# A hybrid encoder on Trainium2: filler moved from first to second half heads of the scan, outputs spread over more places

## The chip, the cores and the metric

One core of a Trainium2 chip runs the whole kernel. TensorE (PE) multiplies and transposes, VectorE (DVE) and ScalarE (ACT) work on elements, GpSimd (POOL) does small vector work and issues some transfers, SyncE (SP) issues most DMAs. The engines run side by side, each through its own queue in order, and wait for each other on semaphores. The metric is the device time of one execution in microseconds, taken as the median of several runs.

## The reference, cut to what matters

One layer over 1024 positions of width 1024: an RMS norm, one combined projection, a convolution mixer and a bidirectional gated recurrence (HGRN2) side by side, their gated merge, and a feed-forward block with a short convolution. The change is in the recurrence, which runs for 8 heads of dimension 128, once forward and once backward:

```python
def step(state, inp):                       # one chunk of positions
    ...
    scores = jnp.einsum("bhtk,bhsk,bhtsk->bhts", qb, kb, decay)
    o = (jnp.einsum("bhts,bhsv->bhtv", scores, vb)
         + jnp.einsum("bhtk,bhkv->bhtv", qb * jnp.exp(a), state))
    ...
o = o_fwd + o_bwd                           # [B,S,H,DV]
of = o * lax.rsqrt(jnp.mean(o * o, axis=-1, keepdims=True) + EPS)
bmix = of * norm_w * jax.nn.silu(og)
```

## The kernel before

Large products run in three float32r passes (L144, L145, L146): each weight page and each activation page is split into a high and a low part, ACT writing the high part (L122) and DVE the low one (L119). The stages follow each other: norm and first projections, convolution beside projections, the recurrence ("the scan", about 530 to 960 us of the profile), output projection and merge, feed-forward, final norm.

**The scan.** It treats each of the 8 heads in two halves of 512 positions (four chunks of 128), first half, then second. In a half:

- `scan_base` (L875) prepares qF and kG, the scaled queries and keys of both directions, with VectorE alone. It is a generator of twelve steps, run a half ahead of use (`ahead`).
- `scan_levels` (L935) joins blocks at four levels, h = 8, 16, 32 and 64. At each, ACT copies keys into A (L945), PE makes eight products, two recorded for each of four chunks (L948), ACT or DVE puts them into the score tile S (L972, L975 to L979, L983), and DVE updates kG and qF for the next level (through `tt`, L840). Level 8 has the products inside the blocks too (L961). A yield follows each level. Ahead of the third place PE transposes v (L1151).
- `scan_states` (L997) transposes kG (L1004; ACT copies the result to kT, L1006), then forms the state contributions u = kT v (L1013) and, on DVE, the forward states Sf (L1021). ACT copies u for the backward states Sb (L1031, L1033). Three yields.

So a half has seven yields, here called **places**, and a head fourteen. At each place `between` does three things in this order: `dense.fill(FILL)`, two steps of the next half's `scan_base`, and one step of `pending`.

- `dense` is the remaining column jobs of the input projection, there to keep PE busy. One column job is eight **pieces** of six products (L144 to L146), then evacuations by ACT (L544, L546) and stores; its weight page is loaded by SP and split by ACT and DVE. `fill(1.3)` adds 1.3 to what is owed and runs one piece for each whole unit, so the seven places of a half bring 9.1 pieces on average. What is left of the jobs after the scan is run behind it.
- `pending` is the generator `outputs` (L1102) of the head before. Its steps are: Sb's recursion, six dependent DVE instructions (L1106); the output products of the first half, 22 on PE into bank "ob" (L1054), copied by ACT (L1056) and squared there (L1059); the same for the second half, then the reciprocal root on POOL (`rstd_small`, L408 and L409); an empty step; the scalings by ACT, four for each half (L1073), in two steps; and for each half four transpositions on PE (L1080), a DVE product with the gate (L1082) and a store. With one step at each place, step k falls in place k of the next head: the last transpositions are done in the first place of its second half. In head 0 there is nothing pending.

**What sets the order.** PE's order is that of the program as written; the other engines' instructions are put in order by the framework's scheduler, from the program's order and its own estimates. PSUM has eight banks: three "mm" for the column jobs, two "sc", two "tr" for transpositions, and one "ob", used by half of level 8's inner products, by half of u, and by the output products. Buffers for a head's states (tag "st") are four, so the next head writes Sf and Sb into the buffers that the outputs read.

After the loop stands a tail written out by hand: calls of `pending.fill` and `dense.fill` for the last head's outputs, and `bm_loads`, which load what the output projection needs.

Of the kernel before, what the change touches and what calls it, by code (L numbers as in the profile page):

```python
# [16 lines left out]
AX = mybir.AxisListType  # L17

P = 128
FILL = 1.3  # L20
CONV_FILL = 1.6
NPAIRS = 17
LN_FILL = 6
# [22 lines left out]
def tile_hybrid_encoder(  # L46
# [45 lines left out]
    def nm(s):  # L92
        uid[0] += 1
        return f"{s}_{uid[0]}"
# [3 lines left out]
    def bank(tag):  # L98
        return ps.tile([P, H], F32, tag=tag, name=nm(tag), bufs=BANKS[tag])

    def page(pool, tag, bufs, dt=F32):
        return pool.tile([P, H], dt, tag=tag, name=nm(tag), bufs=bufs)

    def tmp():
        return page(mp, "tm", 4)

    def ev():
        return page(mp, "ev", 3)

    def hx():  # L110
        return page(mp, "hx", 32, F32R)

    def load(src):
        t = tmp()
        nc.sync.dma_start(t, src)
        return t
# [4 lines left out]
    def split(hi, lo, src, eng):  # L121
        A.copy(hi, src)  # L122
        split_lo(eng, lo, src, hi)
        return hi, lo
# [248 lines left out]
    def vec(key, i):  # L373
        name, o = vec_off[key]
        return vecs[name][:, o + i : o + i + 1]
# [31 lines left out]
    def rstd_small(dst, ss, n):  # L407
        G.tensor_scalar(dst, ss, 1.0 / n, EPS, op0=ALU.mult, op1=ALU.add)  # L408
        G.tensor_tensor(dst, dst, mhalf.to_broadcast(list(dst.shape)), op=ALU.pow)  # L409
# [441 lines left out]
    def scan_inputs(i):  # L851


        h, half = divmod(i, 2)
        q = page(hp, "q", 2)
        f = hp.tile([P, 2, H], F32, tag="f", name=nm("f"), bufs=2)
        kk = hp.tile([P, 2, H], F32, tag="k", name=nm("k"), bufs=2)
        nc.sync.dma_start(q, d_q[h][half])
        for d in range(2):
            z = page(hp, "zi", 3)  # L860
            nc.sync.dma_start(z, d_z[d][h][half])
            A.activation(kk[:, d, :], z, AF.Sigmoid, scale=-1.0)
            A.activation(z, z, AF.Sigmoid)
            fo = view(f, d * H + 7 * d, [[8, NB], [1 - 2 * d, 8]])
            A.activation(
                fo,
                z.rearrange("p (b e) -> p b e", e=8),
                AF.Identity,
                scale=oml_of(d, h),
                bias=lb_of(d, h),  # L870
            )
        V.tensor_scalar(f, f, MIN_FORGET, 1.0, op0=ALU.max, op1=ALU.min)
        return q, f, kk, kscale[:, h : h + NH + 1 : NH]
# [162 lines left out]
    def scan_outputs(h, kept, Sf, Sb):  # L1036


        ons, gates = [], []
        ss = cp.tile([P, 2, 4], F32, name=nm("oss"), tag="oss", bufs=2)  # L1040
        rs = cp.tile([P, 2, 4], F32, name=nm("ors"), tag="ors", bufs=2)
        for half in range(2):
            S_t, v, qF = kept[half]
            o = bank("ob")
            for c in range(4):
                sl = slice(c * P, (c + 1) * P)
                g = half * 4 + c
                terms = [(S_t[:, c, :], v[:, c, :])]
                if g > 0:
                    terms.append((qF[:, 1, sl], Sf[half][:, c, :]))  # L1050
                if g < 7:
                    terms.append((qF[:, 0, sl], Sb[half][:, c, :]))
                for n, (l, r) in enumerate(terms):
                    T.matmul(o[:, sl], l, r, start=(n == 0), stop=(n == len(terms) - 1))  # L1054
            on = tmp()
            A.copy(on, o)  # L1056
            for c in range(4):
                junk = hp.tile([P, DK], F32, tag="jk", name=nm("jk"), bufs=1)
                A.activation(  # L1059
                    junk, on[:, c * P : (c + 1) * P], AF.Square, accum_out=ss[:, half, c : c + 1]  # L1060
                )
            ons.append(on)
            gates.append(page(hp, "og", 2))
            nc.sync.dma_start(gates[half], d_og[h][half])
            if half == 0:
                yield
        rstd_small(rs, ss, DK)
        yield
        yield
        for half in range(2):  # L1070
            for c in range(4):
                sl = slice(c * P, (c + 1) * P)
                A.activation(  # L1073
                    ons[half][:, sl], ons[half][:, sl], AF.Copy, scale=rs[:, half, c : c + 1]
                )
            yield
        for half in range(2):
            b = bank("tr")
            for c in range(4):
                T.transpose(b[:, c * P : (c + 1) * P], ons[half][:, c * P : (c + 1) * P], ident)  # L1080
            bt = ev()
            V.scalar_tensor_tensor(bt, b, vec("hn", h), gates[half], op0=ALU.mult, op1=ALU.mult)  # L1082
            if h == NH - 1:
                bm[h][half] = split(hx(), hx(), bt, V)
            else:
                nc.sync.dma_start(d_bm[h][half], bt)
            yield
# [13 lines left out]

    def outputs(h, kept, Tt, Sf, Sb):  # L1102
        for c in range(5, -1, -1):
            hf, cc = c // 4, c % 4
            n1, c1 = (c + 1) // 4, (c + 1) % 4
            V.scalar_tensor_tensor(  # L1106
                Sb[hf][:, cc, :],
                Sb[n1][:, c1, :],
                Tt[:, n1, 1, c1 : c1 + 1],
                Sb[hf][:, cc, :],  # L1110
                op0=ALU.mult,
                op1=ALU.add,
            )
        yield
        yield from scan_outputs(h, kept, Sf, Sb)
# [11 lines left out]
    pending = Stream(iter(()))  # L1127
    for h in range(NH):
        Tt = hp.tile([P, 2, 2, 4], F32, tag="Tt", name=nm("Tt"), bufs=3)
        Sf = [hp.tile([P, 4, DK], F32, tag="st", name=nm("Sf"), bufs=4) for _ in range(2)]  # L1130
        Sb = [hp.tile([P, 4, DK], F32, tag="st", name=nm("Sb"), bufs=4) for _ in range(2)]
        kept = []
        for half in range(2):
            i = 2 * h + half
            base = cur.result()
            ahead = Base(ins) if i + 1 < NI else None
            ins = scan_inputs(i + 2) if i + 2 < NI else None

            def between(fill):
                dense.fill(fill)  # L1140
                if ahead is not None:
                    ahead.step(BASE_STEPS)
                pending.fill(1)

            S_t = hp.tile([P, 4, P], F32, tag="S", name=nm("S"), bufs=3)
            vl = load(d_v[h][half])
            for n, _ in enumerate(scan_levels(base, S_t, Tt[:, half])):
                if n == 2:
                    b = bank("tr")
                    for c in range(4):  # L1150
                        T.transpose(b[:, c * P : (c + 1) * P], vl[:, c * P : (c + 1) * P], ident)  # L1151
                    v = hp.tile([P, 4, DK], F32, tag="v", name=nm("v"), bufs=3)
                    A.copy(v.rearrange("p c e -> p (c e)"), b)
                between(FILL)
            qF, kG = base[0], base[1]
            for _ in scan_states(i, kG, v, Tt, Sf, Sb):
                between(FILL)
            kept.append((S_t, v, qF))
            cur = ahead
        pending = Stream(outputs(h, kept, Tt, Sf, Sb))  # L1160

    left = 8 * (len(rest) - 2) + 16 - dense.count
    pending.fill(1)
    dense.fill(left - 20)
    pending.fill(1)
    dense.fill(4)
    pending.fill(2)
    dense.fill(4)
    pending.fill(2)
    dense.fill(4)  # L1170
# [323 lines left out]
```

## Time and profile before

| | |
|---|---|
| median of 3 runs | 1859.93 us (1857.55 to 1863.16) |
| the profiled execution | 1873.26 us |
| its span, first to last instruction | 1871.5 us |
| granted TensorE clock, mean | 0.984 of full speed |
| busy: PE, DVE, ACT, POOL | 1788.6, 1275.7, 796.2, 185.8 us |
| matmuls | 8574 |

The profiled execution is one of its own and 13 us longer than the median. Durations below come from it. "Busy" is the time in which an engine had at least one instruction under way; for PE the ends of matmuls are modelled, so its figure is somewhat high. In the views, a wait is written as the waiting engine, tile and line, then the engine, tile and line that released it.

### The profile page before, as it was taken

The page shows a single profiled execution, that of the slowest core. Times are in us where ns is not written, and L with a number is a line of the kernel's source. Part 1 is how long each engine was busy: PE and PEld are TensorE (multiplying, and loading weights), DVE is VectorE, ACT ScalarE, POOL GpSimd, SP SyncE. Part 2 cuts the span into 40 slices and gives each one's busy share as a digit, 9 for nine tenths or more (in the row PEclk, how much of TensorE's full clock was granted, in tenths as well). Part 3 has the DMA queues.
Part 4 walks back from the last instruction along what each step waited for, and adds up shares of the span by engine and source line. Part 5 has one row for each costly group of instructions (what it writes and reads, how often), then busy time and mean ns, then how long its engine had stood idle before and what let it go on. Part 6 is the DMA issues. An engine that isn't in the chain of part 4 may idle for free.

```text
span 1871.5 us, 23768 instructions
## 1 busy us (share of the span) xinstructions
PE 1788.6 (96%) x8574; PEld 1481.4 (79%) x8574; DVE 1275.7 (68%) x1874; ACT 796.2 (43%) x1483; POOL 185.8 (10%) x197
## 2 busy tenths in 40 slices
PE   7989999999999999999989999899999999899996
PEld 6868777777778888888878787688888888788885
DVE  4599999534479999999835565666666667534445
ACT  6443333234545566556442244443444434522124
POOL 1201111213000000000000001111111111000000
PEclk9999999999999999999999999999999999999998
DMA  7658878775653333332238665676776765633134
GB/s 268 213 141 185 184 170 198 184 170 130 208 186 96 113 113 117 98 108 91 74 110 239 191 193 190 152 156 144 150 153 149 156 146 130 208 97 95 55 86 169
DMA packets 323468, 281.42 MB, mean 150 GB/s; under 512 B 14734, under 2 KB 246934, under 8 KB 323350
## 3 DMA queue, kind: packets, MB, share of 16 engines
q1 hardware_dynamic: 272886, 240.05, 41.4%
q0 software_dynamic: 50464, 39.85, 14.9%
q8 instruction: 67, 1.10, 0.3%
q14 instruction: 51, 0.42, 0.1%
HBM read 188.09 MB, written 71.83 MB: 139 GB/s over the span
## 4 chain that ended last, share of the span: by engine, by line
PE 45%; DVE 23%; DMA 18%; ACT 6%; issue 5%; POOL 1%; SPq 0%; ACTq 0%; POOLq 0%; DVEq 0%
PE mm L144 12%; PE mm L145 12%; PE mm L146 12%; DMA wr<-wr 4%; DVE wp L119 3%; DMA wr<-sw 3%; DMA sw<-in_w_in_dram 3%; DMA tm<-d_a 3%; DVE kG L840 2%; DVE acc L755 2%; PE sc L144 2%; PE sc L146 2%; PE sc L145 2%; DVE qF L840 2%; DVE DE L840 2%
## 5 line engine op out<-in xcount | busy, mean ns | idle before, releaser
L144 PE MATMUL mm<-hx,wp 128*128 128x512 f32 x1176 | 480.1, 408 | 23.8 <-DVE ev L541 6.8
L146 PE MATMUL mm<-hx,wp 128*128 128x512 f32 x1176 | 464.9, 395 | 1.9 <-DVE wp L119 1.9
L145 PE MATMUL mm<-hx,wp 128*128 128x512 f32 x1176 | 464.6, 395 | 0.5 <-DVE hx L476 0.5
L122 ACT CAST wp<-wr 128x1024 fp32r<-128x1024 f32 (+2 forms) x193 | 176.7, 915 | 344.8 <-PE mm L145 188.3
L119 DVE TENSOR_TENSOR wp<-wr,wp 128x1024 fp32r<-128x1024 f32 (+2 forms) x193 | 203.4, 1054 | 123.0 <-ACT wp L122 116.2
L144 PEld LDWEIGHTS mm<-hx,wp 128*128 128x128 f32 x1176 | 224.7, 191 | 72.9 <-DVE ev L541 9.7
L146 PEld LDWEIGHTS mm<-hx,wp 128*128 128x128 f32 x1176 | 224.1, 191 | 52.5 <-DVE wp L119 3.7
L145 PEld LDWEIGHTS mm<-hx,wp 128*128 128x128 f32 x1176 | 224.7, 191 | 43.0 <-DVE hx L476 0.8
L755 DVE SCALAR_TENSOR_TENSOR acc<-gl,v_b,acc 128x1024 f32<-128x1024 f32 x120 | 150.0, 1284 | 0.5
L1370 DVE TENSOR_TENSOR xr<-mm,xr 128x512 f32<-128x512 f32 x48 | 33.1, 690 | 80.4 <-PE mm L146 80.4
L948 PE MATMUL sc<-qF,A 128*128 128x128 f32 x512 | 69.8, 280 | 13.3 <-DVE qF L840 13.1
L948 PEld LDWEIGHTS sc<-qF,A 128*128 128x128 f32 x512 | 65.2, 195 | 20.4 <-issue 14.9
L242 POOL DMA_DIRECT2D wr<-sw x38 | 33.8, 889 | 442.8 <-DVE wp L119 153.1
L122 ACT CAST wq<-sw 128x1024 fp32r<-128x1024 f32 x39 | 41.0, 1051 | 77.1 <-PE mm L145 59.5
L945 ACT COPY A<-kG 128x512 f32<-128x512 f32 x64 | 39.6, 618 | 73.8 <-DVE kG L840 51.3
L1292 DVE SCALAR_TENSOR_TENSOR tm<-gp,v_a,tm 128x512 f32<-128x512 f32 x88 | 65.6, 746 | 3.3 <-ACT tm L1288 2.5
L144 PE MATMUL mm<-hy,wp 128*128 128x512 f32 x156 | 62.2, 399 | 3.1 <-ACT su L270 2.9
L145 PE MATMUL mm<-hy,wp 128*128 128x512 f32 x156 | 61.9, 396 | 0.7 <-DVE hy L119 0.7
L270 ACT COPY su<-mm 128x512 f32<-128x512 f32 x78 | 45.1, 578 | 39.2 <-PE mm L146 39.2
L144 PE MATMUL tr<-hx,wp 128*128 128x512 f32 x156 | 61.4, 394 | 0.0
L146 PE MATMUL mm<-hy,wp 128*128 128x512 f32 x156 | 61.1, 392 | 0.0
L144 PE MATMUL sc<-hy,wq 128*128 128x512 f32 x156 | 61.1, 392 | 0.0
(322 smaller groups left out, 3601.5 us busy)
## 6 DMA issues: line engine op xcount, KB each, us to landing
wr<-in_w_in_dram SPq DMA_DIRECT2D x53, 512.0 KB
sw<-in_ffn_w_up_dram SPq DMA_DIRECT2D x44, 256.0 KB
sw<-in_ffn_w_up_dram POOLq DMA_DIRECT2D x22, 512.0 KB, 9.2
wr<-in_ffn_w_up_dram SPq DMA_DIRECT2D x22, 512.0 KB
d_g<-ft SPq DMA_DIRECT2D x44, 256.0 KB
ev<-d_g SPq DMA_DIRECT2D x44, 256.0 KB
wr<-sw POOLq DMA_DIRECT2D x38, 256.0 KB, 3.2
wr<-wr POOLq DMA_DIRECT2D x38, 256.0 KB, 4.8
```

What stands on the lines that cost most here:

```text
L119: eng.tensor_tensor(lo, src, hi.bitcast(F32), op=ALU.subtract)
L122: A.copy(hi, src)
L144: T.matmul(acc, whi[:, k, :], ahi, start=first, stop=False, skip_group_check=again)
L145: T.matmul(acc, whi[:, k, :], alo, start=False, stop=False, skip_group_check=again)
L146: T.matmul(acc, wlo[:, k, :], ahi, start=False, stop=last, skip_group_check=again)
L242: G.dma_start(o, a, accum_op=ALU.add)
L270: A.copy(t, acc)
L755: V.scalar_tensor_tensor(acc, g[:, k : k + S], tap(k), acc, op0=ALU.mult, op1=ALU.add)
L840: V.tensor_tensor(o, a, b, op=op)
L945: A.copy(A_t.rearrange("p (b x e) -> p b x e", x=2, e=h), pairs(kG, h))
L948: T.matmul(b[:, c * P : (c + 1) * P].rearrange("p (b x e) -> p b x e", x=2, e=h), A_t[:, c * P : (c + 1) * P], view(qF, c * P, [[2 * h, P ...
L1292: V.scalar_tensor_tensor(c, g[:, o + k : o + k + H], vec("fdw", k * NF + j), c, op0=ALU.mult, op1=ALU.add,)
```

## The change

Three things. `FILL` becomes a pair, 1.1 for the places of a first half and 1.5 for those of a second. `outputs` yields once within Sb's recursion, after three of its six instructions, so that the recursion takes two places. And the empty steps between the reciprocal root and the scalings become three (four yields in place of two), so that the outputs of a head take eleven of the next head's fourteen places: recursion in places 1 and 2, output products in 3 and 4, nothing in 5 to 7, scalings in 8 and 9, transpositions in 10 and 11. The tail's calls of `pending.fill` are raised by the added steps, and the same work stands between the same calls of `dense.fill` as before.

```diff
-FILL = 1.3
+FILL = (1.1, 1.5)
...
         rstd_small(rs, ss, DK)
-        yield
-        yield
+        for _ in range(4):
+            yield
         for half in range(2):
...
     def outputs(h, kept, Tt, Sf, Sb):
         for c in range(5, -1, -1):
+            if c == 2:
+                yield
             hf, cc = c // 4, c % 4
...
-                between(FILL)
+                between(FILL[half])
             qF, kG = base[0], base[1]
             for _ in scan_states(i, kG, v, Tt, Sf, Sb):
-                between(FILL)
+                between(FILL[half])
...
-    pending.fill(1)
+    pending.fill(2)
     dense.fill(left - 20)
     pending.fill(1)
     dense.fill(4)
-    pending.fill(2)
+    pending.fill(4)
     dense.fill(4)
     pending.fill(2)
     dense.fill(4)
```

## The prediction

> **What bounds the kernel now.** I read the engines' totals first, then the busy time per half head of the scan (the change touches nothing outside it but the order of some hand-written calls behind it), then who makes TensorE wait there, and last the timeline around those waits.
>
> ```profile
> PE 1788.6 (96%) x8574; PEld 1481.4 (79%) x8574; DVE 1275.7 (68%) x1874; ACT 796.2 (43%) x1483; POOL 185.8 (10%) x197
> ```
>
> Over the whole span TensorE (PE) is the bound and VectorE (DVE) is far from it. The scan is different. I cut it at the first level-8 product of each half head; a row has start:end, length, then busy us (and count) of PE, PE's weight loads, DVE, ACT and POOL, the granted clock, DMA share and GB/s. Odd rows are first halves, even ones second halves of heads 0 to 7.
>
> ```profile
> 547.40:573.30 25.90, 23.06 (x132) 19.89 (x131) 23.99 (x42) 10.66 (x19) 0.00 (x0) 0.93 0.35 109
> 573.30:595.70 22.40, 21.36 (x131) 18.48 (x130) 22.33 (x46) 12.36 (x23) 0.00 (x0) 1.00 0.28 87
> 595.70:623.20 27.50, 26.56 (x180) 23.89 (x179) 23.39 (x44) 16.24 (x44) 1.85 (x2) 1.00 0.25 77
> 623.20:647.30 24.10, 21.86 (x137) 18.91 (x136) 23.99 (x43) 13.84 (x25) 0.00 (x0) 1.00 0.46 143
> 647.30:675.20 27.90, 27.02 (x180) 23.91 (x178) 25.31 (x51) 16.45 (x45) 1.87 (x2) 1.00 0.26 85
> 675.20:698.70 23.50, 21.93 (x135) 18.83 (x136) 22.90 (x40) 11.74 (x22) 0.00 (x0) 1.00 0.40 120
> 698.70:726.00 27.30, 26.53 (x179) 23.84 (x178) 25.36 (x51) 17.39 (x46) 2.55 (x2) 1.00 0.35 108
> 726.00:749.60 23.60, 21.66 (x137) 18.87 (x136) 23.18 (x41) 12.66 (x24) 0.00 (x0) 1.00 0.43 136
> 749.60:777.60 28.00, 26.67 (x180) 23.96 (x179) 25.19 (x51) 17.25 (x46) 1.83 (x2) 1.00 0.27 85
> 777.60:804.00 26.40, 24.51 (x142) 21.19 (x141) 24.48 (x45) 11.56 (x22) 0.00 (x0) 0.94 0.37 110
> 804.00:831.80 27.80, 26.76 (x179) 23.77 (x178) 24.60 (x48) 18.00 (x47) 1.84 (x2) 1.00 0.26 86
> 831.80:854.40 22.60, 21.69 (x137) 18.91 (x136) 22.50 (x39) 11.50 (x22) 0.00 (x0) 1.00 0.41 129
> 854.40:882.00 27.60, 26.51 (x180) 23.86 (x179) 24.67 (x48) 17.17 (x46) 1.83 (x2) 1.00 0.21 67
> 882.00:905.10 23.10, 21.61 (x137) 18.85 (x136) 22.97 (x41) 8.77 (x17) 0.00 (x0) 1.00 0.35 116
> 905.10:931.80 26.70, 26.55 (x180) 23.90 (x179) 21.11 (x45) 14.34 (x41) 2.02 (x2) 1.00 0.18 59
> 931.80:955.00 23.20, 21.94 (x138) 18.99 (x136) 13.18 (x24) 6.90 (x13) 0.00 (x0) 1.00 0.35 114
> ```
>
> Take heads 1 to 6, which are alike (595.70 to 905.10, 309.4 us). A first half lasts 27.68 on average, PE is busy 26.68 of it, DVE 24.75, ACT 17.08: PE bounds it, 1.0 us is lost. A second half lasts 23.88, PE is busy 22.21, DVE 23.34, ACT 11.68: DVE bounds it, and PE stands idle 1.7 us. The two halves have different bounds, and each leaves the other engine's time unused. All that PE loses in these heads is 6 x (1.0 + 1.7) = 16.1 us; that is the ceiling of what any reordering can win there.
>
> Who PE waits for between 595 and 905 (total us, times, longest), and two waits of ACT between 547 and 955:
>
> ```profile
> PE sc L948 <- DVE qF L840: 8.8, 8, 1.9
> PE sc L1013 <- ACT kT L1006: 5.5, 6, 1.3
> PE sc L961 <- ACT Sb L1031: 1.5, 1, 1.5
> ```
>
> ```profile
> ACT k L862 <- DVE Kh L843: 15.4, 8, 3.9
> ACT tm L1073 <- POOL ors L409: 9.2, 7, 1.6
> ```
>
> The three rows sum to 15.8 us, the same idle time seen from the other side. The second occurs six times, once per first half. The timeline of head 2's first half shows its origin:
>
> ```profile
> 670.25 1.28 ACT L1073 ACTIVATE tm<-tm,ors 128x128 f32<-128x128 f32 x4 [1.37 <-POOL ors L409]
> 671.44 0.56 ACT L1006 COPY kT<-tr 128x512 f32<-128x512 f32 x1
> 672.97 1.23 DVE L119 TENSOR_TENSOR wp<-wr,wp 128x1024 fp32r<-128x1024 f32 x1 [2.49 <-ACT wp L122]
> ```
>
> ACT stands 1.37 us at the output scaling (L1073) until POOL has the reciprocal root, spends 1.28 us on four scalings, and only then copies kT, for which PE waits; a weight page behind it on ACT is late too, and DVE idles 2.49 us for that.
>
> **The change part by part.** Durations (us busy, mean ns; the last row min/median/max ns):
>
> ```profile
> L1106 DVE SCALAR_TENSOR_TENSOR Sb<-Sb,Tt 128x128 f32<-128x128 f32 x38 | 13.1, 344 | 0.5 <-ACT Sb L1031 0.3
> L1082 DVE SCALAR_TENSOR_TENSOR ev<-tr,v_a,og 128x512 f32<-128x512 f32 x14 | 10.4, 744 | 1.7 <-PE tr L1080 1.7
> L119 DVE TENSOR_TENSOR wp<-wr,wp 128x1024 fp32r<-128x1024 f32 x18 | 21.9, 1219 | 7.0 <-ACT wp L122 7.0
> L1073 ACT ACTIVATE tm<-tm,ors 128x128 f32<-128x128 f32 x56 | 17.9, 391 | 9.2 <-POOL ors L409 9.2
> L1056 ACT COPY tm<-ob 128x512 f32<-128x512 f32 x14 | 8.1, 577 | 9.4 <-PE ob L1054 9.4
> L409 POOL TENSOR_TENSOR ors<-ors,mhalf x8: 1633/1634/1669, 616.9 to 964.5; 128x8 f32<-128x8 f32 x8
> ```
>
> What PE does around level 32 in a first half (head 1), with the DVE update that this level needs, and in a second half (head 4):
>
> ```profile
> 599.79 1.05 PE L948 MATMUL sc<-qF,A 128*128 128x128 f32 x8
> 600.60 0.47 PE L144 MATMUL mm<-hx,wp 128*128 128x512 f32 x1
> 602.02 0.67 DVE L840 TENSOR_TENSOR qF<-qF,tb 128x512 f32<-128x512 f32 x1
> 602.07 0.38 PE L1054 MATMUL ob<-v,S 128*128 128x128 f32 x2
> 604.52 1.06 PE L948 MATMUL sc<-qF,A 128*128 128x128 f32 x8
> ```
>
> ```profile
> 783.04 0.60 PE L1080 MATMUL tr<-ident,tm 128*128 128x128 f32 x4
> 783.47 1.06 PE L948 MATMUL sc<-qF,A 128*128 128x128 f32 x8
> 787.81 1.13 PE L948 MATMUL sc<-qF,A 128*128 128x128 f32 x8 [1.89 <-DVE qF L840]
> 790.08 0.63 PE L146 MATMUL mm<-hx,wp 128*128 128x512 f32 x1
> ```
>
> *Filler.* Per half 1.3 x 7 = 9.1 pieces become 1.1 x 7 = 7.7 and 1.5 x 7 = 10.5; a head keeps 18.2, so the scan's total, and what is left for the tail, stay. A piece is six products, 600.60 to 602.07 = 1.47 us, or about 1.4 where it follows another. So 1.4 pieces, 1.95 us of PE, move. A column job has eight pieces and one DVE subtraction of 1.22 us (L119): 0.21 us of DVE moves with them, and the jobs' loads and stores move on SP's queue with their piece, whose DMA share here is 0.18 to 0.46.
>
> *Turning the outputs (places 10 and 11).* Before, one transposition block was in the last place of a first half and one in the first of a second; now both are in the second, places 3 and 4. That moves 783.04 to 783.47 = 0.43 us of PE and one L1082, 0.74 us of DVE.
>
> *Scalings (places 8 and 9).* Eight go from the end of a first half to the start of a second: two groups of 1.28 us, 2.6 us of ACT. POOL's 1.63 us now has three empty places ahead of its reader; even three single pieces are 4.4 us, so the 1.37 us wait on POOL should go. If POOL were later than that, the wait would come back at the second half's first levels.
>
> *Sb's recursion.* Six steps of 0.34 us stay six; three go one place later, so up to 1.0 us of DVE moves from ahead of level 16 to ahead of level 32. The output products, which read Sb, go a place later too.
>
> *New per half, heads 1 to 6.* First half: PE 26.68 - 1.95 - 0.43 = 24.3, DVE 24.75 - 0.74 - 0.21 = 23.8, ACT 17.08 - 2.6 = 14.5 or a little less. Second half: PE 22.21 + 2.38 = 24.6 (24.1 without the half at 777.60, which has a slow clock), DVE 23.34 + 0.95 = 24.3, ACT 14.3. Both halves are balanced; neither engine has two us to spare any more. What is lost above the busiest engine is 1.0 us now in a first half (27.68 - 26.68) and 0.5 in a second (23.88 - 23.34). With two engines level, it can't be less; from 0.5 to the 2.7 us that PE loses per head now are the bounds per half. I take 1.0 for a first half (its kT wait goes, a wait at level 32 comes) and 0.5 for a second: 25.3 + 25.1 = 50.4 against 51.56, 1.2 us a head, 7 us in six heads.
>
> *Where cover is lost.* In a first half the 22 output products (602.07 to 604.52, 2.45 us) stood between level 16 and level 32; now they stand behind level 32, and mostly one piece of 1.4 us is left as cover. DVE's update began at 602.02, 0.67 long: with the level wanted at 602.1 instead of 604.5, PE would wait some 0.6 us here, up to 1.9 as in the second halves. In a second half both L1082 (1.5 us of DVE) and, on average, one filler piece less stood ahead of level 32; I expect the 1.89 us waits there to go mostly. I cost this pair at +0.8 and -1.2 us a head; it lies within the sums above.
>
> *New waits.* The two output blocks share one ob bank and are now only level 64 (0.8 us, as level 16 from 599.79 to 600.60) and one piece apart: the copy L1056 (0.58 us) must leave ACT within some 2.3 us, and ACT has waits of up to 3.9 us (L862) that could stand ahead of it. Behind it wait PE's second block, and all that follows on PE. In places 3 to 6 of a second half, v's, two output and two kT transpositions take the two tr banks in turn: kT then waits for L1082 on DVE. Bounds: nothing, to 1.3 us a head (the longest wait for kT now). I take nothing for the tr banks, as two places lie between, and 0.2 us for ob.
>
> *Heads 0 and 7.* Head 0 has no outputs to spread. Its first half loses two pieces, but is late through DVE (23.99 of 25.90): -0.3; its second gains two, PE 21.36 + 2.8 = 24.2, with 0.5 lost 24.7 against 22.40: +2.3. In head 7 DVE has room in both halves (21.11, 13.18), PE sets both, and work only changes sides: 0. The tail has the same order on PE.
>
> *The slow spell.* After the 1.89 us wait at 787.81 a product takes 0.63 us (790.08) where 0.47 and less is usual, and that half's granted clock is 0.94; the other second halves of heads 1 to 6 have 1.00. Its PE time is 24.51 against 21.75 on average in the other five, and the sums above carry these 2.8 us. I take it that the wait brought the spell and that both go: -2.8. An execution that had no such spell before gains that much less.
>
> Sum: -7.0 + 0.2 x 6 + 2.0 - 2.8 = **-6.6 us**. The profiled execution took 1873.26 us, its span and 1.8 us around it; the median of the runs shown is 1859.93. The scan's rows hold for both, so 1873.26 becomes 1866.7, and the median 1859.93 - 6.6 = **1853 us**.
>
> **The rivals.** *The slow spell stays* (1856): if a wait as short as 1.89 us doesn't slow the clock, the spell at 790 has another cause and comes again; -6.6 + 2.8 = -3.8. For it: seven of the eight waits for qF between 595 and 905 are followed by no spell. The Trainium skill ("TensorE: Matmul & The Clock Gate", "Part 1: The HAM clock gate") has the clock halve after about 3.4 us of idling, and by that page waits of this length cost no clock. The trace agrees in those seven places and not in the one.
>
> *Balanced and none the better* (1859): two level engines wait for each other as much as before, 2.7 us of PE a head, only elsewhere; six heads then give nothing, and head 0's +2 and the spell's -2.8 leave -1. For it: now an engine with 1.9 us of room (26.68 against 24.75) stands beside the bound one in a first half, and none after. Against it: kT's wait has a cause that is removed. *The change doesn't reach its waits* belongs here: if kT is held up by the squares of the second block, which now stand one place later, instead of the scalings, 5.5 us stay.
>
> *Level 32 in first halves* (1867): DVE must do Sb's six steps, 2.06 us, ahead of that level as before, but PE arrives 2.45 us earlier. If DVE enters a first half no earlier than now, PE waits 8.8 / 8 = 1.1 (the mean wait for qF, mostly in second halves) + 2.06 = 3.2 us there, first half 24.3 + 3.2 = 27.5, second 24.6 + 0.5 = 25.1: 52.6 against 51.56, +6; with head 0's +2.0 and a half of the spell's -2.8, +7. It decides once PE's waits pass 2.7 us a head. Against it: a second half's DVE is no longer the bound by 1.6 us, so it should enter the next first half earlier.
>
> *Most of PE's idle time goes* (1846): 0.5 us lost in each half, first 24.3 + 0.5, second 24.6 + 0.5: 49.9 a head, 1.66 less, -10; with head 0's +2.0 and the spell's -2.8, -11, and up to -14 where DVE's late start in head 0 goes too.
>
> **How the numbers follow.** A measurement of this kernel tells 0.3% (5.6 us) from no change. Forecast 0.32, most idle time goes 0.22, the spell stays 0.06, balanced 0.20, level 32 0.20. The forecast's own spread reaches to about -4, so 0.02 of it lies within 0.3%: faster 0.32 + 0.22 - 0.02 = 0.52, within 0.3% 0.06 + 0.20 + 0.02 = 0.28, slower 0.20. The range takes in all five: from 1841 (all of the 16.1 us and the spell gone, head 0 as above: -17, and 2 us more for the runs' own spread) to 1868 (level 32).
>
> **What would show it.** Right: rows of first and second halves within 1 us of each other, near 25; no row of L1073 waiting for POOL in the scan; PE's wait for kT under 2 us in all, for qF under 9 spread over both halves; DVE over 0.95 busy in both. Wrong: first halves still at 27 with qF waits at level 32; L1054 waiting for L1056, or L1004 for L1082; ACT's copies of kT still late.

## The result and the profile after

| | before | after |
|---|---|---|
| median of 5 runs | 1861.05 us (1857.55 to 1864.15) | 1880.14 us (1873.10 to 1882.42) |
| ratio | | 1.0096 [1.0071, 1.0120] |
| profiled execution, its span | 1873.26, 1871.5 us | 1878.54, 1876.8 us |

The changed kernel is slower. On a second occasion (run e5 below) the same two kernels gave 1.0051 [1.0033, 1.0069], 9.7 us. I cut the two traces at the first inner product of the scan (L961) and its last state product (L1013): the scan takes 404.3 us before and 413.4 after, 9.1 more. What comes behind it takes about 919 in both; over the profiles of all kernels here that part, whose work is the same, lies between 903 and 919. So about 9 us are the scan's, by one profile of each kernel, and the other 9 or 10 of the first occasion are not explained by any row that I found.

The engines' totals of after, which hardly differ from those of before:

```profile
PE 1787.7 (95%) x8574; PEld 1477.7 (79%) x8574; DVE 1280.1 (68%) x1874; ACT 795.1 (42%) x1483; POOL 185.7 (10%) x197
```

The half heads of heads 1 to 6 of after, cut and read as the prediction's view of before (first halves in the odd rows):

```profile
590.00:616.80 26.80, 24.93 (x163) 22.41 (x163) 24.97 (x50) 14.34 (x37) 1.74 (x2) 0.94 0.29 89
616.80:644.60 27.80, 25.07 (x151) 21.59 (x150) 25.39 (x46) 16.14 (x33) 0.10 (x1) 1.00 0.34 105
644.60:672.80 28.20, 26.32 (x170) 23.54 (x169) 23.00 (x43) 14.26 (x39) 2.03 (x2) 0.94 0.27 84
672.80:698.20 25.40, 23.48 (x145) 20.47 (x144) 24.36 (x42) 14.24 (x30) 0.00 (x0) 1.00 0.44 139
698.20:724.90 26.70, 24.72 (x169) 22.27 (x169) 25.25 (x51) 14.21 (x38) 1.83 (x2) 1.00 0.30 95
724.90:750.80 25.90, 23.76 (x146) 20.53 (x145) 23.27 (x42) 14.72 (x31) 0.00 (x0) 1.00 0.37 123
750.80:776.50 25.70, 25.01 (x169) 22.21 (x168) 24.51 (x50) 13.66 (x37) 1.83 (x2) 1.00 0.28 93
776.50:804.00 27.50, 25.08 (x151) 21.58 (x150) 24.99 (x46) 14.82 (x32) 0.00 (x0) 1.00 0.35 106
804.00:828.10 24.10, 23.36 (x163) 21.18 (x162) 23.34 (x44) 13.51 (x37) 1.83 (x2) 1.00 0.31 100
828.10:855.30 27.20, 25.02 (x151) 21.58 (x151) 25.12 (x44) 16.17 (x33) 0.00 (x0) 1.00 0.31 107
855.30:880.00 24.70, 23.37 (x164) 21.17 (x163) 23.71 (x48) 13.60 (x36) 1.13 (x2) 1.00 0.19 64
880.00:910.60 30.60, 27.81 (x151) 24.09 (x150) 25.76 (x48) 11.27 (x25) 1.43 (x1) 0.89 0.29 95
```

The mean of six rows of a kind: a first half lasts 26.0 us with PE busy 24.6, DVE 24.1, ACT 13.9; a second half 27.4 with 25.0, 24.8 and 14.6. The work moved as forecast (24.3, 23.8, 14.5 and 24.6, 24.3, 14.3). The loss above PE did not: 1.4 us in a first half (1.0 forecast) and 2.4 in a second (0.5 forecast). The six heads take 320.6 us instead of 309.4. Who PE waits for there (between 588 and 908), and ACT's wait for POOL in the whole scan (540 to 960):

```profile
PE sc L948 <- DVE qF L840: 10.4, 7, 2.0
PE sc L961 <- ACT Sb L1031: 9.4, 6, 2.7
PE sc L948 <- ACT ev L544: 1.4, 1, 1.4
PE tr L1004 <- ACT kT L1006: 0.8, 1, 0.8
PE sc L1013 <- ACT kT L1006: 0.6, 1, 0.6
```

```profile
ACT tm L1073 <- POOL ors L409: 12.2, 7, 2.3
```

The kT waits are gone (0.6 of 5.5 us), as forecast. In their place stands a row that was 1.5 us, once: the inner products of level 8 wait for the copy of Sb, 9.4 us in six. And the wait on POOL, which the prediction saw go, grew from 9.2 to 12.2. All rows sum to 22.6 us, and PE's idle time in the six heads is 22.7, against 16.1 before. These 6.6 us, and 4.6 us more of busy PE, most of it in the three rows with a clock below 1.00, make the 11.2.

The timeline of after at the end of head 1's first half (start, duration, engine, line; in brackets the idle time ahead), in ACT's order of issue:

```profile
614.47 0.33 ACT L1059 ACTIVATE jk<-tm 128x128 f32<-128x128 f32 x1
614.77 0.62 ACT L945 COPY A<-kG 128x512 f32<-128x512 f32 x1
616.93 1.28 ACT L1073 ACTIVATE tm<-tm,ors 128x128 f32<-128x128 f32 x4 [1.54 <-POOL ors L409]
618.12 0.60 ACT L945 COPY A<-kG 128x512 f32<-128x512 f32 x1
618.62 0.47 ACT L1031 COPY Sb<-sc 128x384 f32<-128x384 f32 x1
619.00 1.28 ACT L1073 ACTIVATE tm<-tm,ors 128x128 f32<-128x128 f32 x4
```

```profile
614.55 1.06 PE L1013 MATMUL sc<-v,kT 128*128 128x128 f32 x8
616.82 1.05 PE L948 MATMUL sc<-qF,A 128*128 128x128 f32 x8
619.14 1.16 PE L961 MATMUL sc<-Qh,Kh 128*128 128x128 f32 x8 [1.27 <-ACT Sb L1031]
```

The scalings (L1073) stand right behind the squares (L1059) and one copy, not three places later. ACT waits there for POOL, does four scalings and one more copy of A, and only then copies Sb out of the "sc" bank that PE filled at 614.55. That bank is the next that PE needs, for the inner products of level 8 (the other holds L948): PE stands 1.27 us.

### The profile page after: what moved, and what is told of

Read it like the earlier page. It is cut to its first block, busy times and chain, and to the rows that moved or that the text cites. A ratio compares the mean times of both kernels' runs of the same rounds, so it can differ in the third digit from the quotient of the medians.

```text
span 1876.8 us, 23778 instructions
## 1 busy us (share of the span) xinstructions
PE 1787.7 (95%) x8574; PEld 1477.7 (79%) x8574; DVE 1280.1 (68%) x1874; ACT 795.1 (42%) x1483; POOL 185.7 (10%) x197
## 4 chain that ended last, share of the span: by engine, by line
PE 44%; DMA 22%; DVE 19%; ACT 8%; issue 5%; POOL 1%; SPq 0%; ACTq 0%; POOLq 0%; DVEq 0%
PE mm L144 11%; PE mm L145 11%; PE mm L146 11%; DMA wr<-wr 4%; DMA wr<-sw 4%; DVE wp L119 3%; DMA sw<-in_w_in_dram 3%; DMA tm<-d_a 3%; DVE acc L755 2%; DMA sw<-in_ffn_w_up_dram 2%; PE sc L144 1%; PE sc L146 1%; PE sc L145 1%; DMA wr<-in_w_in_dram 1%; DVE kG L840 1%
## 5 line engine op out<-in xcount | busy, mean ns | idle before, releaser
L144 PEld LDWEIGHTS mm<-hx,wp 128*128 128x128 f32 x1176 | 224.2, 191 | 73.4 <-DVE ev L541 10.1
L948 PEld LDWEIGHTS sc<-qF,A 128*128 128x128 f32 x512 | 64.8, 191 | 25.4 <-issue 11.3
L948 PE MATMUL sc<-qF,A 128*128 128x128 f32 x512 | 68.7, 277 | 16.6 <-DVE qF L840 14.6
L144 PE MATMUL mm<-hy,wp 128*128 128x512 f32 x156 | 61.3, 393 | 4.6 <-ACT su L270 4.6
L145 PE MATMUL mm<-hy,wp 128*128 128x512 f32 x156 | 61.2, 392 | 0.0
L144 PE MATMUL sc<-hy,wq 128*128 128x512 f32 x156 | 61.0, 391 | 0.0
L146 PE MATMUL sc<-hy,wq 128*128 128x512 f32 x156 | 60.9, 391 | 0.0
L145 PE MATMUL sc<-hy,wq 128*128 128x512 f32 x156 | 60.7, 389 | 0.0
```

The source lines that it names most:

```text
L144: T.matmul(acc, whi[:, k, :], ahi, start=first, stop=False, skip_group_check=again)
L145: T.matmul(acc, whi[:, k, :], alo, start=False, stop=False, skip_group_check=again)
L146: T.matmul(acc, wlo[:, k, :], ahi, start=False, stop=last, skip_group_check=again)
L948: T.matmul(b[:, c * P : (c + 1) * P].rearrange("p (b x e) -> p b x e", x=2, e=h), A_t[:, c * P : (c + 1) * P], view(qF, c * P, [[2 * h, P ...
```

## The experiments

The change has three parts, here F (the filler pair), R (the yield in Sb's recursion) and Y (four yields in place of two, the empty places). Two theories stood against each other after the result. By the first, the new order uncovers level 32: PE comes to it early and waits for qF. By the second, nothing has moved the scalings on ACT, and their wait on POOL now holds up the copy of Sb instead of the copy of kT. The runs came in four groups, each timed beside the kernel before, whose medians were 1860.00, 1858.29, 1862.06 and 1858.99 us. Lengths of the scan are cut as above, PE's waits lie between 540 and 960 us.

### The parts alone, and the whole again

**e1, F alone.**

```diff
-FILL = 1.3
+FILL = (1.1, 1.5)
...
-                between(FILL)
+                between(FILL[half])
```

> Only the filler pair (1.1 in first halves, 1.5 in second ones); outputs as before. Theory COVER (the loss comes from the output products leaving place 2, which bares level 32 in first halves, and from ACT's scalings, whose wait for POOL then stands ahead of the copy of Sb at the start of second halves): the products still cover level 32, so no loss, 1853 to 1863 us. Rival FILLER (first halves now lack filler, which is what lets PE wait): slower by 10 us or more, 1871 to 1880.

Measured: 1.0007 [0.9987, 1.0027], scan 403.8. PE's waits in the trace:

```profile
PE sc L1013 <- ACT kT L1006: 11.2, 6, 2.7
PE sc L948 <- DVE qF L840: 7.1, 7, 2.8
```

The waits for qF fall from 13.1 us to 7.1, and those for kT double: first halves have less filler ahead of kT. What F gains in second halves, where most of the waits for qF were, it loses in first ones, where all the waits for kT are.

**e2, R alone.**

```diff
         for c in range(5, -1, -1):
+            if c == 2:
+                yield
...
-    pending.fill(1)
+    pending.fill(2)
```

> Only Sb's recursion in two places, so that every later step of the outputs stands one place later (products in places 3 and 4); filler 1.3 throughout, two yields ahead of the scalings. COVER: most of the loss is here, 1872 to 1882, with waits for qF in first halves and waits of level 8's inner products for the copy of Sb in second halves, 8 to 10 us in all. FILLER: within 4 us of 1861.

Measured: 1.0040 [1.0019, 1.0061], scan 410.0.

```profile
PE sc L948 <- DVE qF L840: 14.3, 13, 2.8
PE sc L961 <- ACT Sb L1031: 6.5, 6, 1.5
```

R alone brings most of the loss, and with it the row of Sb; ACT waits for POOL 12.0 us in seven. The outputs and their squares come one place later, and the wait behind them too: past the copies of kT, ahead of that of Sb.

**e3, Y alone.**

```diff
-        yield
-        yield
+        for _ in range(4):
+            yield
...
-    pending.fill(2)
+    pending.fill(4)
```

> Only four yields in place of two ahead of the scalings; recursion in one place, filler 1.3. COVER: ACT's order is hardly touched by the yields, the scalings still stand behind the squares and wait for POOL some 1.3 us in each head; only the transpositions move to places 2 and 3 of second halves. 1857 to 1866. Rival BANKS (the transpositions between level 16 and kT in second halves are the loss, through the tr banks or DVE): 1870 or more.

Measured: 0.9991 [0.9972, 1.0010], scan 403.0.

```profile
PE sc L948 <- DVE qF L840: 6.9, 8, 2.8
PE sc L1013 <- ACT kT L1006: 6.2, 5, 3.5
```

```profile
ACT tm L1073 <- POOL ors L409: 9.9, 6, 2.7
```

Here the step of the prediction stands by itself: two more empty places between root and scalings, and ACT waits for POOL as long as before (9.9 us against 9.2), and PE for kT (6.2 against 5.6).

**e4, R and Y; e6, F and R; e5, the whole change once more.**

> Recursion in two places and four yields, filler 1.3: the change without its filler pair. COVER: 1872 to 1884, as recursion alone. FILLER: 1858 to 1864.

> Filler pair and recursion in two places, two yields ahead of the scalings. Theory PAIR (the filler pair leaves one piece in place 2 of first halves just where the products were taken away, so level 32 waits 1 to 2 us in every head): as the whole change, 1.007 to 1.012. Rival ADD (the parts are independent): 1.004 to 1.005.

> The changed kernel a second time, beside the next three. So far filler alone gave 1.0007 of the time before, recursion alone 1.0040, empties alone 0.9991, recursion and empties 1.0027. If the parts simply add, the whole is 1.003 to 1.005; if filler and the later products hurt each other, it is 1.008 to 1.012 again.

Measured: e4 1.0027 [1.0006, 1.0048], e6 1.0035 [1.0017, 1.0054], e5 1.0051 [1.0033, 1.0069]; scans 411.0, 409.8 and 411.4. The intervals overlap: each of these kernels with R loses some 0.3 to 0.5%, and what stands beside it decides little. The sizes that were expected of R were too large: e2 and e4 were put at 1872 us or more and came out at 1866.37 and 1865.53, and e6 lies below what either side expected. The trace of e5 repeats that of after, with 9.3 us in six for Sb.

### The wait on POOL taken away, and level 32 covered

**e7, after, with scalings that do not read POOL's result.** The output of the recurrence is then not normalized; instructions and counts stay.

```diff
-                    ons[half][:, sl], ons[half][:, sl], AF.Copy, scale=rs[:, half, c : c + 1]
+                    ons[half][:, sl], ons[half][:, sl], AF.Copy, scale=ones_m[:, c : c + 1]
```

> The changed kernel with the scalings reading a constant in place of POOL's reciprocal root, so the recurrence's output is not normalized; all instructions stay. If ACT's wait for POOL ahead of the copy of Sb causes the waits at the start of second halves (9.4 us in six), these go, and the time falls by 6 to 10 us against the changed kernel. Rival: the squares and scalings themselves (some 4 us of ACT a head) make the copy late; then 0 to 3 us.

Measured: 0.9955 [0.9935, 0.9976], scan 399.9, 17.7 us under e5 on the same occasion (1867.94 - 1850.27), where 6 to 10 were expected. The two profiles show 11.5 of them in the scan (411.4 to 399.9). The granted clock of the runs differs too, 0.990 at the median against 0.9875, so not all of the 17.7 need be the waits themselves.

```profile
PE sc L948 <- DVE qF L840: 16.5, 12, 2.8
PE sc L961 <- ACT Sb L1031: 0.3, 1, 0.3
```

The row of Sb is gone with its cause, and the sign of the change turns, although the waits for qF are longer than in after.

**e8, after, with one piece more ahead of level 32 in first halves and half a piece less in two later places.** Lines stand one lower in its trace.

```diff
+COVER = (0, 1, 0, 0, 0, -0.5, -0.5)
...
-                between(FILL[half])
+                between(FILL[half] + (0.0, COVER[n])[half == 0])
```

> The changed kernel with one filler piece more in place 2 of every first half and half a piece less in places 6 and 7, so that two pieces stand between level 16 and level 32. PAIR: the waits for qF in first halves (9 to 10 us in all) fall to under 3 and the time by 5 to 9 us. Rival BEHIND (DVE is behind anyway, and the wait comes back at level 64 or at kT): within 3 us of the changed kernel.

Measured: 1.0044 [1.0018, 1.0070], scan 412.6.

```profile
PE sc L962 <- ACT Sb L1032: 10.5, 6, 3.5
PE sc L949 <- DVE qF L841: 7.0, 8, 1.7
```

Half of the qF waits went and no time with them, as the rival had it. PE's rows sum to 27.7 us where those of e5 sum to 28.1: what goes for qF (7.7 us) comes back for Sb (1.2), for kT at the state products (3.5), and in smaller rows. e7 and e8 together decide against the first theory as the driver.

### An earlier root

**e9, after, with one reciprocal root for each output block, issued right behind its squares.** The first block's root is then done a place before it is read.

```diff
+            rstd_small(rs[:, half, :], ss[:, half, :], DK)
             ons.append(on)
...
-        rstd_small(rs, ss, DK)
```

> The changed kernel with one reciprocal root for each output block, issued behind that block's squares, in place of one for both; all that the reference asks is computed, with two POOL instructions more a head. Theory POOL (ACT's in-order wait for POOL's root is what the change turned from a kT wait into a longer one ahead of the copy of Sb; without it the changed kernel ran 0.9955 of the time before): the first four scalings no longer wait, the last four only for what the first four do not cover; 0.996 to 0.999. Rival: the wait only moves to the second block's scalings: 1.003 to 1.006.

Measured: 0.9950 [0.9926, 0.9974], 1853.05 us, scan 401.4. This kernel computes the whole reference and is faster than the kernel before and the changed one.

```profile
PE sc L948 <- DVE qF L840: 16.5, 12, 2.8
PE sc L961 <- ACT Sb L1031: 0.3, 1, 0.3
```

ACT waits for POOL 2.3 us in two, and in its timeline the scalings stand where they stood, with nothing in brackets:

```profile
617.09 1.28 ACT L1073 ACTIVATE tm<-tm,ors 128x128 f32<-128x128 f32 x4
618.27 0.61 ACT L945 COPY A<-kG 128x512 f32<-128x512 f32 x1
618.78 0.47 ACT L1031 COPY Sb<-sc 128x384 f32<-128x384 f32 x1
```

**e10, before with that root; e12, F with it; e15, R and Y with it (filler 1.3).** Their diffs are those above.

> The kernel before with one root for each output block, nothing else. POOL: kT's waits (5.6 us in seven) mostly go; 0.995 to 0.998. Rival (first halves were bound by PE alone, and the kT waits were hidden behind other lateness of DVE): 0.999 to 1.001.

> Filler pair and one root for each block, recursion and places as before. With the filler pair alone the kT waits were longest (11.2 us in six), so the root should be worth most here: 0.991 to 0.996, the fastest of the correct kernels. Rival: less filler in first halves lets the other waits there grow instead: 0.998 to 1.002.

> The changed kernel without the filler pair (1.3 throughout), with one root for each block. With the pair it was 0.9950. If the pair is worth something once the wait for POOL is gone: 0.997 to 1.000; if it costs or does nothing: 0.992 to 0.996.

Measured: e10 1.0017 [0.9998, 1.0036], e12 1.0046 [1.0031, 1.0062], e15 0.9953 [0.9929, 0.9977]; scans 409.5, 418.3 and 398.1. e15 equals e9: with the root early, F gives nothing that the time shows, though ACT waits for POOL 8.0 us in e15 and 2.3 in e9. e10 and e12 were misses: the early root alone does no good. In e10 ACT waits longer, not less:

```profile
ACT tm L1073 <- POOL ors L409: 20.7, 12, 7.1
```

```profile
659.79 6.09 POOL L409 TENSOR_TENSOR ors<-ors,mhalf 128x4 f32<-128x4 f32 x1
...
665.91 1.28 ACT L1073 ACTIVATE tm<-tm,ors 128x128 f32<-128x128 f32 x4 [7.06 <-POOL ors L409]
```

In this order the scheduler puts the first block's scalings right behind the squares, and one root lasted 6.09 us. In e12 ACT waits 27.0 us in twelve; its roots (shortest, median and longest in ns):

```profile
L409 POOL TENSOR_TENSOR ors<-ors,mhalf x16: 1006/1008/6167, 604.4 to 977.1; 128x4 f32<-128x4 f32 x16
```

### The wait on POOL taken away without R, and the scalings held

**e11, before, with scalings that do not read POOL's result; e14, R alone with them.** The edit is that of e7, and what is left out too. In both, the scheduler also put the first four scalings earlier, right behind or among their squares; in e7 they stand in front of the copy of Sb, as in after.

> The kernel before with the scalings reading a constant in place of POOL's root, so its recurrence output is not normalized. It bounds what the wait costs before. POOL: 0.993 to 0.997, that is 6 to 13 us, less than the 17 us it was worth in the changed kernel. If it comes out as low as the changed kernel without the wait (0.9955), the change's own shift of work brings nothing; if higher, the shift is worth the difference.

> The kernel before with the recursion in two places and the scalings reading a constant (its recurrence output is not normalized). Without the wait for POOL the kernel before ran at 0.9921 and the changed one at 0.9955, so 0.0034 remain. If the later output products carry them (level 32 in first halves without cover), this is 0.994 to 0.997; if the filler pair or the empty places carry them, 0.991 to 0.993.

Measured: e11 0.9921 [0.9899, 0.9943], scan 392.3; e14 0.9926 [0.9901, 0.9951], scan 394.8. With the POOL wait in, R costs 0.4% (e2); without it, nothing. So with filler at 1.3, R's later output products, and with them the lost cover of level 32, cost nothing that these intervals (0.25% either way) show. The wait is worth some 0.8% of the kernel before, and 1.0% of the changed one (1.0051 - 0.9955); for the kernel before that is more than the 6 to 13 us expected, and part of it may be the new order of the scalings in e11.

**e13, after, with the scalings held on ACT behind the copy of S at level 8.** The edit constrains the scheduler's order and nothing else: it is the order that the prediction had taken for granted.

```diff
-                A.copy(S_t, b)
+                mark[0] = A.copy(S_t, b)
...
+                with tc.issue_after(mark[0].ins):
                     A.activation(
```

> The changed kernel with its scalings bound, in issue order alone, behind ACT's copy of S at level 8 of the second half, which is where the prediction believed that the empty places put them. Theory ORDER (the empty places bind nothing: the scheduler issues the scalings as soon as it thinks them ready, in front of the copy of Sb, and there ACT waits for POOL): without other change the wait for POOL and the waits for the copy of Sb go, and the time is 0.994 to 0.998 of that before. Rival LOAD (it is ACT's load at the start of second halves, wherever the scalings stand): 1.002 to 1.006, with waits for A at level 16 in their place.

Measured: 0.9965 [0.9941, 0.9989], 1855.48 us, scan 401.3. Lines stand two or three lower in its trace. PE's longest row of waits, ACT's wait for POOL, and ACT's order in head 1:

```profile
PE sc L950 <- DVE qF L840: 16.7, 12, 2.8
```

```profile
ACT tm L1076 <- POOL ors L409: 2.0, 1, 2.0
```

```profile
616.27 0.62 ACT L947 COPY A<-kG 128x512 f32<-128x512 f32 x1 [0.76 <-DVE kG L840]
616.79 0.47 ACT L1033 COPY Sb<-sc 128x384 f32<-128x384 f32 x1
618.02 0.59 ACT L974 COPY S<-sc 128x512 f32<-128x512 f32 x1 [0.76 <-PE sc L950]
618.50 2.45 ACT L1076 ACTIVATE tm<-tm,ors 128x128 f32<-128x128 f32 x8
```

The copy of Sb starts at 616.79 instead of 618.62, no wait for Sb is left, and the kernel is 0.35% faster than before. So the cause is the place of the scalings in ACT's order: in front of the copy of Sb they wait for POOL, and the copy waits with them.

## Why the prediction was wrong

The forecast was 1853 us, and the time lies above its range. **The step that failed** is that of the scalings: "POOL's 1.63 us now has three empty places ahead of its reader; [...] so the 1.37 us wait on POOL should go." The yields are places in the program, and only PE runs in the program's order. The description of the kernel says that the scheduler orders the other engines; the prediction counted places for ACT all the same. The scheduler put the scalings at the first spot at which it took them for ready, right behind the squares, with at most one copy between in heads 1 to 6. e3 shows it with the empty places alone, e13 shows what the intended order is worth: 1855.48 of 1858.99 us, -3.5, where the prediction had -6.6. The prediction had named where the wait would come back, "at the second half's first levels", if POOL were late; POOL took 1.63 us as before, and it was the reader that came too early.

**The size that came of it.** The second half's 0.5 us of loss became 2.4, of which 1.6 are one row: 9.4 us in six heads for Sb. R moved the squares one place, so the wait left kT and fell upon Sb; a wait whose cause stays moves with its neighbours. The rival "the change doesn't reach its waits" named a related cause, the squares, and put its price at kT's 5.5 us; the price was another, since what was held up changed.

**Right:** the pieces moved (each half's busy time to 0.6 us), the kT waits went, in heads 1 to 6 the waits for qF fell from 8.5 to 2.6 us in second halves and rose from 0.3 to 7.8 in first ones. Their sum in the whole scan barely moved: 13.1 us before, 14.6 after. That was the rival "level 32 in first halves", right as to the place, but e7, e8 and e14 do not let it be the main cause. L1004 never waited for L1082, as costed, and no row of after shows PE waiting for the copy out of ob (L1056), costed at 0.2 us a head.

**The slow spell.** The half that follows 777 has its full clock again, as forecast (776.50, 27.50 us long), and others have lost theirs: 0.94, 0.94 and 0.89 in the rows at 590.00, 644.60 and 880.00. So the 2.8 us did not come back as a gain. Each of the three spells begins right behind a wait of PE, two behind waits for qF of 1.87 and 1.88 us (at 598.43 and 653.01), the last behind the longest wait for Sb:

```profile
883.68 2.07 PE L961 MATMUL sc<-Qh,Kh 128*128 128x128 f32 x8 [2.67 <-ACT Sb L1031]
```

In that half PE is busy 27.81 us where the three others with as many products (x151) have 25.02 to 25.08, so if the wait brought the spell, it cost an estimated 2.8 us more than its own length. Waits of 1.92, 1.98 and 2.77 us in the same scan have no such spell behind them, so the length alone does not decide. The Trainium skill ("TensorE: Matmul & The Clock Gate", "Part 1: The HAM clock gate") asks for about 3.4 us of idling before the clock halves. The longest wait of PE in this scan is 2.8 us, so the trace does not agree.

**Balanced halves** show no gain here: F is 1.0007 alone, and e9 and e15, with it and without it, are equal.

**Open.** The first occasion's loss was twice the second's, and no run explains that; the granted clock was 0.983 to 0.987 in its five runs and 0.985 to 0.989 in the ten of e5, so part of it may lie there. Without the wait on POOL the changed kernel (e7) lies 0.0034 above the kernel before (e11), with intervals that overlap slightly, and e11's order was not quite that of before; whether the change costs a little besides the wait is not settled. If it does, e14 (0.9926) points at the filler pair or the empty places: PE waits for qF 16.5 us in e7 and 10.1 in e14, which has R without them.

## What to carry to other kernels

A place written by hand orders only the engine whose order is taken from the program: look up in the timeline where the instructions of the other engines stand before counting on a gap. A wait on an in-order queue costs what is queued behind it, so its length alone says little; ask which copies it will stand ahead of after the change. To remove it, move its producer earlier (e9) or hold its reader (e13), and look up in the new timeline where both have landed: with the early root alone (e10, e12) the reader moved forward too, and waited longer than before.

## What the runs showed of the hardware

POOL's root on 128x4 elements takes 1.01 us at the median and took up to 6.09 in e10 and 6.17 in e12. On VectorE, instructions stood back to back in the time of the first, all but one short copy with two inputs; the first and the last of them, and the one behind, in the trace of e10:

```profile
659.58 0.73 DVE L843 SCALAR_TENSOR_TENSOR Kh<-k,kscale,DE 128x512 f32<-128x512 f32 x1
...
664.94 0.41 DVE L840 TENSOR_TENSOR DE<-DE,f 128x128 f32<-128x128 f32 x1
665.38 1.76 DVE L896 RECIPROCAL DE<-DE 128x256 f32<-128x256 f32 x1
```

POOL's instruction ended at 665.88, 0.5 us after this reciprocal, which has one input, had begun. The Trainium skill ("GPSIMD Engine Reference", "1. Specifications") has POOL share its SBUF interfaces with VectorE, with contention where VectorE reads two inputs. The trace agrees, with a factor of six. No run here took VectorE's work away to show it, so the cause is argued.
